# Key and value columns of the compressed branch, computed between the transposes of x, in a one-core Hymba-style decoder step

## Chip, core and metric

One core of a Trainium2 chip runs the whole step as one program. The metric is the device time of one execution in microseconds (us), the median over repeated runs. TensorE (PE in the profile) does matrix products and transposes, VectorE (DVE) and ScalarE (ACT) do elementwise work, GpSimd (POOL) does elementwise work and issues gathers, and SyncE (SP) issues most DMA transfers. Each engine works through its own list of instructions in order and waits on semaphores for the others.

## What is computed

The reference is one layer of a hybrid decoder for 1024 prompt tokens and for 8 samples of 4 new tokens, 1056 tokens in all. Cut to what the change touches:

```python
u = rmsnorm(x, lw['norm_mix'])            # x (tokens, 1024): u = x * r * norm_mix, r one number per token
z = u @ w_in                              # 2328 columns: q | k_cmp | v_cmp | k_slc | v_slc | ... | rg | rx
kc = compress(concat(cache k_cmp, k_cmp)) # blocks of 32 tokens, a small MLP per block; the same for v_cmp
h, conv_state, h_last = rglru(rx, ...)    # convolution, two gates, a linear scan over time
x = x + concat(rmsnorm(attention), rmsnorm(gelu(rg) * h)) @ w_out
v = rmsnorm(x, lw['norm_mlp'])
x = x + square(relu(v @ w_up)) @ w_down
```

`k_cmp` and `v_cmp` are columns 512 to 639 and 640 to 767 of `w_in`.

## The kernel before, in words

Tokens lie along the free axis in three chunks of 352 columns (`CH`), features along the 128 partitions. Every large product is done with three matmuls (`mm3`, lines 122 to 124), since both factors are split into a high and a low part (`split`, lines 127 and 128): high by high, high by low, low by high. An input projection of 128 columns is therefore 3 chunks of 8 blocks of features of 3 matmuls, 72 in all, and each writes 128x352.

**The start.** `fetch_x` loads x in nine tiles of up to 128 tokens (`xt`, line 276, eight buffers). `load_x` takes them in three groups of three tiles. For each of the 8 blocks of features (`kb`) it transposes the three tiles on TensorE into one PSUM tile `ps_x` (line 257), ScalarE writes the high part `u_hi` (line 261), VectorE the low part `u_lo` (line 262) and one of the two a plain copy `xr` (line 265), which GpSimd's queue stores. The factor r per token is not in u; `norm_x` builds it as a row `R` over all tokens (line 1168 makes diagonals `dg`, line 1169 broadcasts them with TensorE into `ps_bc`, line 1171 copies), and each projection multiplies its result by `R` when it leaves PSUM.

**Then, before the change:** `z_tile` runs twice, for the columns of k_cmp and of v_cmp, all three chunks of the one and then of the other. `cmp_cached` compresses the cached pages: for 4 pairs of samples and k, v it takes page data `lpg` (half loaded by SP, line 547, half gathered by GpSimd's queue, line 551; 16 tiles in three buffers), reorders it into `lpr` (line 586), transposes it on TensorE (`ps_ct`, line 593), splits it into `xj0` (k) or `xj1` (v) on ScalarE and VectorE (lines 508 and 509) and multiplies by the compression weights (`ps_c`). `kv_cmp` does the same for the new rows, and `rglru` follows.

**Weights.** `w_tile` loads 512 KB of `w_in` into `wraw` (line 299, one buffer) and splits it into `wh`, `wl`, of which there are two sets, used in turn. So the load of a third tile can be split only when the first tile's last matmul is done, and the load after that can start only when that split is done.

```python
raw = self.wrp.tile([128, KT, 128], F32, tag="wraw", name="wraw", bufs=1)
self.wp = self.wps[self.par]
self.par ^= 1
```

**Order.** The program is written with a tile library whose scheduler, at build time, sets the order on each engine from a model of the durations; the order in which the code emits operations is only a priority. `w_tile` raises it.

**Two later places.** `rglru` ends with a transpose `ps_l` of its last states (line 411). In the first eighth of the MLP, `scale_x1` sums squares of x per chunk on ScalarE and GpSimd, adds over partitions on TensorE (`ps_ms`, line 1227), makes `dg` on VectorE (line 1238), broadcasts (`ps_bc`, line 1239) and multiplies x by the result (line 1338).

Of the kernel before, what the change touches and what calls it, by code (L numbers as in the profile page):

```python
# [9 lines left out]
F32 = mybir.dt.float32  # L10
# [8 lines left out]
D = 1024  # L19
# [86 lines left out]
class K:  # L106
# [130 lines left out]
    def load_x(self):  # L237
# [7 lines left out]
        for grp in range(3):  # L245
# [6 lines left out]
            for kb in range(KT):  # L252
                pool, tag = ((self.ps_tp, "tp"), (self.ps_mm, "mm"))[kb % 2]
                ps = pool.tile([128, 512], F32, tag=tag, name="ps_x")
                o = 0
                for xt, n in tiles:
                    nc.tensor.transpose(ps[:, o : o + n], xt[:n, kb * 128 : kb * 128 + 128], self.ident[:n, :n])
                    o += n
                g = self.g_mix[:, kb : kb + 1]
                hi, lo = uh[:, kb, c0 : c0 + wdt], ul[:, kb, c0 : c0 + wdt]  # L260
                nc.scalar.activation(hi, ps[:, :wdt], AF.Copy, scale=g)
                nc.vector.scalar_tensor_tensor(lo, ps[:, :wdt], g, hi.bitcast(F32), ALU.mult, ALU.subtract)
                if kb % 2 == 0:
                    xr = self.xrp.tile([128, 2, 384], F32, tag="xr", name="xr", bufs=5)
                (nc.scalar.copy if kb % 4 == 0 else nc.vector.tensor_copy)(xr[:, kb % 2, :wdt], ps[:, :wdt])
                if kb % 2:
                    self.stores[grp, kb] = nc.gpsimd.dma_start(self.xT[kb - 1 : kb + 1, :, c0 : c0 + wdt].rearrange("k p t -> p k t"), xr[:, :, :wdt])

    def fetch_x(self):
# [3 lines left out]
        for t in range(9):  # L273
            n = 128 if t < 8 else 32
            xt = self.xtp.tile([128, D], F32, tag="xt", name="xt", bufs=8)
            nc.sync.dma_start(xt[:n], a["x_prompt"][0, t * 128 : t * 128 + 128] if t < 8 else xs)
# [28 lines left out]
    def in_proj(self, c0, evac, order=range(NCH)):  # L305
# [3 lines left out]
        for c in order:  # L309
            ps = self.ps_mm.tile([128, 512], F32, tag="mm", name="ps_in")  # L310
            sl = slice(c * CH, c * CH + CH)
            for k in range(KT):
                self.mm3(ps[:, :CH], wh[:, k], wl[:, k], uh[:, k, sl], ul[:, k, sl], k == 0, k == KT - 1)
            evac(c, ps[:, :CH])

    def z_tile(self, c0, pool, tag, bufs, scale=None, w=TOK):
# [38 lines left out]
    def rglru(self, f, c_rx):  # L355
# [52 lines left out]
        P.tensor_copy(lt[:, 27:28], h[:, SEQ - 1 : SEQ])  # L408
        P.tensor_copy(lt[:, 28:36], hs[:, :, 3])
        ps = self.ps_tp.tile([128, 512], F32, tag="tp", name="ps_l")  # L410
        nc.tensor.transpose(ps[:36, :128], lt, self.ident)
        V.tensor_copy(self.last[:, f * 128 : f * 128 + 128], ps[:36, :128])
        return h

    def rg_gate(self, f, c_rg, h):

        V, S = self.nc.vector, self.nc.scalar
        rp = self.rp
        hs = h[:, SEQ:XC].rearrange("p (s w) -> p s w", w=7)[:, :, 3:7]
        z = self.z_tile(c_rg, self.rx, "X", 4, w=XW)  # L420
        q = rp.tile([128, TOK], F32, tag="gq", name="gq", bufs=1)
        S.activation(q, z, AF.Square, scale=0.044715 ** 0.5)
# [785 lines left out]

    def chunk_ms(self, pool, xs, nf, c, ps, name):

        nc = self.nc
        acc = pool.tile([128, CH], F32, tag="sq", name="sq", bufs=3)
        for f, x in enumerate(xs):
            if f == 0:
                nc.scalar.activation(acc, x, AF.Square)
            else:
                t = pool.tile([128, CH], F32, tag="sq", name="sqt", bufs=3)
                nc.scalar.activation(t, x, AF.Square)
                nc.gpsimd.tensor_tensor(acc, acc, t, ALU.add)
        return self.sum_ms(acc, nf, ps, name)  # L1220

# [104 lines left out]

    def scale_x1(self, c):

        nc = self.nc
        x1 = self.x1  # L1330
        sl = slice(c * CH, c * CH + CH)
        pool = self.scp
        new = lambda nm: self.ps_tp.tile([128, 512], F32, tag="tp", name=nm)
        ms = self.chunk_ms(pool, [x1[:, d, sl] for d in range(8)], D, c, new("ps_ms"), "ms_v")
        M = pool.tile([128, CH], F32, tag="M", name="M", bufs=1)
        self.chunk_bcast(ms, new("ps_bc"), M)
        for d in range(8):
            nc.vector.tensor_tensor(x1[:, d, sl], x1[:, d, sl], M, ALU.mult)
        nc.vector.scalar_tensor_tensor(self.eps2[:, c], ms, D * EPS, ms, ALU.mult, ALU.mult)

    def mlp(self, PP, WU):
# [16 lines left out]
        def down(d, c, ws, hs):  # L1358
# [5 lines left out]
            V.tensor_tensor(x1[:, d, sl], x1[:, d, sl], ps[:, :CH], ALU.add)  # L1364

        for g in range(8):
            hs = []
            for fi in range(4):
                wh, wl = up_w(g * 4 + fi)
                if g == 0 and fi:  # L1370
                    self.scale_x1(CO[fi - 1])
                hh = hp.tile([128, TOK], F32R, tag="hh", name="hh", bufs=4)
                hl = hp.tile([128, TOK], F32R, tag="hl", name="hl", bufs=4)
                for c in (CO if g == 0 else range(NCH)):
# [6 lines left out]
                    V.tensor_tensor(r, r, r, ALU.mult)  # L1381
                    self.split(hh[:, sl], hl[:, sl], r)
                hs.append((hh, hl))
            ws = []
# [85 lines left out]
    def run(self):  # L1470
# [10 lines left out]
        with ExitStack() as PA:  # L1481
# [3 lines left out]
            with ExitStack() as s:  # L1485
# [3 lines left out]
                self.wrp = self.pool(WB, "wrp", side="right")  # L1489
                self.par = 0  # L1490
                with ExitStack() as s2:
                    self.xtp = self.pool(s2, "xtp")
# [7 lines left out]
                    self.vectors()  # L1500
                self.zp = self.pool(s, "zp")
                self.ctp0 = self.pool(s, "ctp0", 1)
                self.ctp1 = self.pool(s, "ctp1", 1)
                self.rowp0 = self.pool(s, "rowp0", 1)
                self.norm_x()
                zs = [self.z_tile(512 + i * 128, self.zp, "z", 2) for i in range(2)]
                self.cmp_cached()
                self.kv_cmp(zs)
        with ExitStack() as PB:
# [128 lines left out]
```

## Time and profile before

| what | value |
|---|---|
| median of 3 runs | 1540.94 us (1536.79 to 1542.21) |
| the profiled execution | 1544.62 us, its span 1542.9 us |
| TensorE busy | 1468.0 us, 95% of the span, 9445 matmuls |
| VectorE, ScalarE, GpSimd busy | 58%, 40%, 28% |
| granted TensorE clock, mean | 0.973 of full speed |

The profile comes from one execution. Times in rows are microseconds from the start of its span unless marked ns. A row of the timeline has start, duration, engine, line and operation, and in brackets the idle time before it and what released it. The duration of a matmul includes its way through the array, so its pace is read from the distance of two starts. The granted clock of TensorE is 1.00 at 2.4 GHz and 0.50 at 1.2 GHz.

### The profile page before, as it was taken

The page shows a single profiled execution, that of the slowest core. Times are in us where ns is not written, and L with a number is a line of the kernel's source. Part 1 is how long each engine was busy: PE and PEld are TensorE (multiplying, and loading weights), DVE is VectorE, ACT ScalarE, POOL GpSimd, SP SyncE. Part 2 cuts the span into 40 slices and gives each one's busy share as a digit, 9 for nine tenths or more (in the row PEclk, how much of TensorE's full clock was granted, in tenths as well). Part 3 has the DMA queues.
Part 4 walks back from the last instruction along what each step waited for, and adds up shares of the span by engine and source line. Part 5 has one row for each costly group of instructions (what it writes and reads, how often), then busy time and mean ns, then how long its engine had stood idle before and what let it go on. Part 6 is the DMA issues. An engine that isn't in the chain of part 4 may idle for free.

```text
span 1542.9 us, 24576 instructions
## 1 busy us (share of the span) xinstructions
PE 1468.0 (95%) x9445; PEld 1378.4 (89%) x9445; DVE 895.2 (58%) x1671; ACT 615.1 (40%) x1216; POOL 439.6 (28%) x533
## 2 busy tenths in 40 slices
PE   4989999999899989999999999999999999999997
PEld 3879998899877657777999999999999999999997
DVE  6664788557678868988786343433424343342445
ACT  6253775122467758767362030311203031130322
POOL 6651143342566648756580000000000000000022
PEclk8899999999789999999999999999999999999999
DMA  9554412453134100003221020511102021020102
GB/s 291 160 160 114 128 33 63 143 186 106 42 105 142 42 1 1 28 1 126 83 69 42 16 81 15 188 31 54 57 8 89 14 70 40 28 81 3 42 23 90
DMA packets 127961, 115.53 MB, mean 75 GB/s; under 512 B 16752, under 2 KB 115760, under 8 KB 127716
## 3 DMA queue, kind: packets, MB, share of 16 engines
q1 hardware_dynamic: 122446, 102.10, 21.8%
q0 software_dynamic: 3200, 8.67, 1.8%
q10 hardware_dynamic: 2198, 3.20, 0.7%
q8 instruction: 74, 1.21, 0.3%
q14 instruction: 43, 0.35, 0.1%
HBM read 98.17 MB, written 28.32 MB: 82 GB/s over the span
## 4 chain that ended last, share of the span: by engine, by line
PE 54%; DVE 4%; ACT 1%; POOL 1%; issue 1%; DMA 0%; DVEq 0%; ACTq 0%; POOLq 0%
PE ps_dn L122 8%; PE ps_dn L123 8%; PE ps_dn L124 8%; PE ps_up L122 7%; PE ps_up L123 7%; PE ps_up L124 7%; PE ps_T L1092 2%; PE ps_O L1101 1%; PE ps_O L1102 1%; PE ps_S L1060 1%; PE ps_S L1061 1%; PE ps_out L122 1%; PE ps_out L124 1%; PE ps_out L123 1%; PE ps_f L1433 0%
## 5 line engine op out<-in xcount | busy, mean ns | idle before, releaser
L122 PE MATMUL ps_up<-v_hi,wuh 128*128 128x352 f32 x768 | 248.9, 324 | 0.0
L122 PE MATMUL ps_dn<-hh,wdh 128*128 128x352 f32 x768 | 248.4, 324 | 0.0
L123 PE MATMUL ps_up<-v_lo,wuh 128*128 128x352 f32 x768 | 247.2, 322 | 0.0
L124 PE MATMUL ps_up<-v_hi,wul 128*128 128x352 f32 x768 | 246.9, 321 | 0.0
L123 PE MATMUL ps_dn<-hl,wdh 128*128 128x352 f32 x768 | 246.0, 322 | 0.0
L124 PE MATMUL ps_dn<-hh,wdl 128*128 128x352 f32 x768 | 245.7, 321 | 0.0
L1364 DVE TENSOR_TENSOR x<-x,ps_dn 128x352 f32<-128x352 f32 x192 | 99.1, 520 | 222.6 <-PE ps_dn L124 222.4
L1429 POOL TENSOR_TENSOR facc<-facc,fsq 128x352 f32<-128x352 f32 x18 | 17.0, 942 | 701.8 <-ACT fsq L1427 701.6
L127 ACT CAST wdh<-wd 128x1024 fp32r<-128x1024 f32 x32 | 33.5, 1048 | 342.2 <-PE ps_dn L123 288.7
L123 PEld LDWEIGHTS ps_up<-v_lo,wuh 128*128 128x128 f32 x768 | 145.0, 189 | 0.0
L122 PEld LDWEIGHTS ps_up<-v_hi,wuh 128*128 128x128 f32 x768 | 144.6, 188 | 0.0
L124 PEld LDWEIGHTS ps_up<-v_hi,wul 128*128 128x128 f32 x768 | 144.5, 188 | 0.0
L123 PEld LDWEIGHTS ps_dn<-hl,wdh 128*128 128x128 f32 x768 | 144.3, 188 | 0.0
L122 PEld LDWEIGHTS ps_dn<-hh,wdh 128*128 128x128 f32 x768 | 144.1, 188 | 0.0
L124 PEld LDWEIGHTS ps_dn<-hh,wdl 128*128 128x128 f32 x768 | 144.0, 188 | 0.0
L122 PE MATMUL ps_in<-u_hi,wh 128*128 128x352 f32 x432 | 142.0, 329 | 0.0
L124 PE MATMUL ps_in<-u_hi,wl 128*128 128x352 f32 x432 | 140.6, 326 | 0.0
L123 PE MATMUL ps_in<-u_lo,wh 128*128 128x352 f32 x432 | 140.4, 325 | 0.0
L128 DVE TENSOR_TENSOR ptl<-ps_T,pth 128x512 fp32r<-128x512 f32 x132 | 88.1, 683 | 16.3 <-ACT pth L127 14.9
L127 ACT CAST pth<-ps_T 128x512 fp32r<-128x512 f32 (+1 forms) x148 | 84.1, 586 | 30.7 <-PE ps_T L1092 25.2
L127 ACT CAST hh<-r 128x352 fp32r<-128x352 f32 x96 | 46.7, 487 | 92.3 <-DVE r L1381 91.5
L122 PEld LDWEIGHTS ps_in<-u_hi,wh 128*128 128x128 f32 x432 | 82.4, 191 | 0.6 <-issue 0.3
(511 smaller groups left out, 3266.7 us busy)
## 6 DMA issues: line engine op xcount, KB each, us to landing
wu<-in_w_up_dram SPq DMA_DIRECT2D x32, 512.0 KB
wd<-in_w_down_dram SPq DMA_DIRECT2D x32, 512.0 KB
wraw<-in_w_in_dram SPq DMA_DIRECT2D x18, 512.0 KB
slc_dram<-in_cache_kv_dram SPq DMA_DIRECT2D x64, 128.0 KB
kvs<-slc_dram SPq DMA_DIRECT2D x32, 256.0 KB
xres<-xT_dram SPq DMA_DIRECT2D x8, 528.0 KB
x_dram<-xres SPq DMA_DIRECT2D x8, 528.0 KB
x<-x_dram SPq DMA_DIRECT2D x3, 1408.0 KB
```

The lines of the kernel that those rows point to most:

```text
L122: t.matmul(out, wh, xh, start=first, stop=False)
L123: t.matmul(out, wh, xl, start=False, stop=False)
L124: t.matmul(out, wl, xh, start=False, stop=last)
L127: self.nc.scalar.copy(hi, src)
L128: (eng or self.nc.vector).tensor_tensor(lo, src, hi.bitcast(F32), ALU.subtract)
L1060: T.matmul(pv, qr[:, h], kh[:, ks], start=True, stop=False)
L1061: T.matmul(pv, qr[:, h], kl[:, ks], start=False, stop=not (far or dia))
L1092: T.transpose(ps[:K, h * 128 : h * 128 + 128], src(h), self.ident)
L1101: T.matmul(O, v, ph, start=first, stop=False)
L1102: T.matmul(O, v, pl, start=False, stop=last)
L1364: V.tensor_tensor(x1[:, d, sl], x1[:, d, sl], ps[:, :CH], ALU.add)
L1429: P.tensor_tensor(acc, acc, sq, ALU.add)
```

## The change

`kv_chunk(c)` computes chunk c of both tiles. Chunks 0 and 1 are emitted after the second and third group of transposes, copied out of PSUM by ScalarE without R, and multiplied by R on GpSimd later, 704 columns at once; chunk 2 comes where the two `z_tile` calls were. The result pool `zp` is opened earlier, the x tiles get six buffers in place of eight, and half of the transposes use the PSUM pool `ps_c` in place of `ps_mm`. Apart from that, `ps_l` is emitted in the next stage, and `scale_x1` becomes a generator whose steps are emitted one per chunk of the MLP's first products.

```diff
-                pool, tag = ((self.ps_tp, "tp"), (self.ps_mm, "mm"))[kb % 2]
+                pool, tag = ((self.ps_tp, "tp"), (self.ps_c, "c"))[kb % 2]
...
+            if grp:
+                self.kv_chunk(grp - 1)
...
-            xt = self.xtp.tile([128, D], F32, tag="xt", name="xt", bufs=8)
+            xt = self.xtp.tile([128, D], F32, tag="xt", name="xt", bufs=6)
...
+    def kv_chunk(self, c):
+
+        nc = self.nc
+        if c == 0:
+            self.wkv = [self.w_tile(512 + i * 128, 128) for i in range(2)]
+            self.zkv = [self.zp.tile([128, TOK], F32, tag="z", name="z", bufs=2) for _ in range(2)]
+        uh, ul = self.u
+        sl = slice(c * CH, c * CH + CH)
+        for z, (wh, wl) in zip(self.zkv, self.wkv):
+            ps = self.ps_mm.tile([128, 512], F32, tag="mm", name="ps_in")
+            for k in range(KT):
+                self.mm3(ps[:, :CH], wh[:, k], wl[:, k], uh[:, k, sl], ul[:, k, sl], k == 0, k == KT - 1)
+            if c < 2:
+                nc.scalar.copy(z[:, sl], ps[:, :CH])
+            else:
+                nc.vector.tensor_tensor(z[:, sl], ps[:, :CH], self.R[:, sl], ALU.mult)
+                nc.gpsimd.tensor_tensor(z[:, : 2 * CH], z[:, : 2 * CH], self.R[:, : 2 * CH], ALU.mult)
...
-                zs = [self.z_tile(512 + i * 128, self.zp, "z", 2) for i in range(2)]
+                self.kv_chunk(2)
                 self.cmp_cached()
-                self.kv_cmp(zs)
+                self.kv_cmp(self.zkv)
...
+        for c in CO:
+            sl = slice(c * CH, c * CH + CH)
+            acc = self.squares(pool, [x1[:, d, sl] for d in range(8)])
+            yield
+            yield
+            ms = self.sum_ms(acc, D, new("ps_ms"), "ms_v")
+            yield
...
+        steps = self.scale_x1()
...
-                if g == 0 and fi:
-                    self.scale_x1(CO[fi - 1])
...
+                    if g == 0 and (fi or c != CO[0]):
+                        next(steps, None)
```

What the scheduler makes of it is seen in the order of the instructions. The order differs up to the gates of the attention and in the first eighth of the MLP; in the attention between them it is the same.

On TensorE at the start (`ps_x` are transposes of x, `ps_in` the columns of k_cmp and v_cmp), before and then changed:

```order
L257 MATMUL ps_x<-ident,xt 128x128 x2
L170 MATMUL ps_gm<-ident,gm 128x8
L257 MATMUL ps_x<-ident,xt 128x128 x2
L459 MATMUL ps_pe<-ident,pe 128x16
L257 MATMUL ps_x<-ident,xt 128x128 x6
L459 MATMUL ps_pe<-ident,pe 128x16
L525 MATMUL ps_pg<-pf_143,tok 128x32
L257 MATMUL ps_x<-ident,xt 128x128 x35
```

```order
L257 MATMUL ps_x<-ident,xt 128x128 x8
L549 MATMUL ps_pg<-pf_146,tok 128x32
L257 MATMUL ps_x<-ident,xt 128x128 x5
L122 MATMUL ps_in<-u_hi,wh 128x352
L123 MATMUL ps_in<-u_lo,wh 128x352
L124 MATMUL ps_in<-u_hi,wl 128x352
L122 MATMUL ps_in<-u_hi,wh 128x352
L123 MATMUL ps_in<-u_lo,wh 128x352
L124 MATMUL ps_in<-u_hi,wl 128x352
L122 MATMUL ps_in<-u_hi,wh 128x352
L257 MATMUL ps_x<-ident,xt 128x128 x3
L123 MATMUL ps_in<-u_lo,wh 128x352
```

Before, all 72 transposes stand ahead of the first `ps_in`; now matmuls begin after 15 transposes and alternate with them to the end of x: 18 matmuls and 18 transposes, then 26 matmuls in a row, and so on.

On ScalarE at the end of the x stage (`wh` is the high part of the next weight tile, `xj0h` and `xj1h` the high parts of the first cached k and v), before and then changed:

```order
L127 CAST wh<-wraw 128x1024
L508 CAST xj1h<-peT 128x8x2
L1171 COPY R<-ps_bc 128x32
L508 CAST xj1h<-ps_ct 128x8x2x32 x2
L508 CAST xj0h<-ps_ct 128x8x2x32
L127 CAST wh<-wraw 128x1024
L508 CAST xj1h<-ps_ct 128x8x2x32 x2
```

```order
L532 CAST xj0h<-ps_ct 128x8x2x32 x3
L127 CAST wh<-wraw 128x1024
L1195 COPY R<-ps_bc 128x512
L222 ACTIVATE sp_w<-sp_w 128x4
L1195 COPY R<-ps_bc 128x32
L127 CAST wh<-wraw 128x1024
L532 CAST xj1h<-peT 128x8x2
L532 CAST xj1h<-ps_ct 128x8x2x32 x2
L532 CAST xj0h<-ps_ct 128x8x2x32
```

The two `wh` casts, with the four `xj0h` casts ahead of the second before, now follow each other closely, and the fourth `xj0h` stands behind both.

On SP, where the loads of weight tiles 4 and 5 (`wraw`) stand among the page loads (`lpg`), before and then changed:

```order
L547 DMA lpg<-in_cache_kv_dram 64x2x256
L299 DMA wraw<-in_w_in_dram 128x8x128
L537 TENSOR_LOAD pt
L537 ISA x2
L537 TENSOR_LOAD pt
L537 ISA x2
L547 ISA
L547 DMA lpg<-in_cache_kv_dram 64x2x256
```

```order
L561 TENSOR_LOAD pt
L561 ISA x2
L301 DMA wraw<-in_w_in_dram 128x8x128 x2
L571 ISA
L571 DMA lpg<-in_cache_kv_dram 64x2x256
```

Before, 14 page loads stand ahead of the first of these two `wraw` and 20 ahead of the second; now 12 stand ahead of both, and the other 20 behind.

## Rows read from the trace of the kernel before

**Rows 1.** The page, part 1: busy time, share of the span, instructions.

```profile
PE 1468.0 (95%) x9445; PEld 1378.4 (89%) x9445; DVE 895.2 (58%) x1671; ACT 615.1 (40%) x1216; POOL 439.6 (28%) x533
```

**Rows 2.** Stretches: length, busy by engine (instructions), then TensorE's clock, DMA share, GB/s.

```profile
14.90:43.40 28.50, 16.27 (x67) 11.11 (x67) 26.62 (x71) 21.78 (x46) 20.17 (x25) 0.64 1.01 268
43.40:47.00 3.60, 3.60 (x14) 3.60 (x13) 3.60 (x16) 1.53 (x2) 3.11 (x6) 0.50 1.03 285
47.00:73.30 26.30, 25.50 (x167) 24.98 (x167) 13.29 (x30) 4.58 (x9) 15.94 (x20) 1.00 0.44 138
...
833.00:1500.00 667.00, 667.00 (x4204) 666.86 (x4203) 251.89 (x439) 138.42 (x236) 6.32 (x7) 1.00 0.16 48
```

**Rows 3.** What TensorE waited for, 0 to 45 us: total, times, longest.

```profile
PE ps_x L257 <- issue: 6.0, 1, 6.0
PE ps_x L257 <- DVE xr L265: 4.4, 5, 1.8
```

**Rows 4.** Timeline of TensorE, first 75 us.

```profile
13.56 1.33 PE L257 MATMUL ps_x<-ident,xt 128*128 128x128 f32 x5
...
31.98 4.13 PE L257 MATMUL ps_x<-ident,xt 128*128 128x128 f32 x15 [5.99 <-issue]
...
44.10 0.49 PE L124 MATMUL ps_in<-u_hi,wl 128*128 128x352 f32 x1
...
46.16 0.49 PE L122 MATMUL ps_in<-u_hi,wh 128*128 128x352 f32 x1
...
73.32 1.04 PE L593 MATMUL ps_ct<-ident,lpr 128*128 128x128 f32 x8
74.11 0.37 PE L122 MATMUL ps_c<-xj0h,cwkh 128*128 128x258 f32 x1
```

**Rows 5.** Timeline of ScalarE: a weight cast, casts of cached rows, and a cast in the MLP.

```profile
73.35 1.05 ACT L127 CAST wh<-wraw 128x1024 fp32r<-128x1024 f32 x1 [6.88 <-PE ps_in L123]
74.31 1.07 ACT L508 CAST xj1h<-ps_ct 128x512 fp32r<-128x512 f32 x2
...
975.13 1.05 ACT L127 CAST wdh<-wd 128x1024 fp32r<-128x1024 f32 x1 [4.87 <-DMA wd<-in_w_down_dram]
```

**Rows 6.** Timeline of VectorE: a small multiply, and the split of a weight tile.

```profile
28.34 3.50 DVE L211 TENSOR_SCALAR hb<-vec 128x8 f32<-128x8 f32 x1
...
61.28 1.22 DVE L128 TENSOR_TENSOR wl<-wraw,wh 128x1024 fp32r<-128x1024 f32 x1 [0.42 <-ACT wh L127]
```

**Rows 7.** Timeline of SP's DMA issues.

```profile
50.57 4.12 SPq L547 DMA_DIRECT2D lpg<-in_cache_kv_dram  x4
62.53 0.41 SPq L299 DMA_DIRECT2D wraw<-in_w_in_dram  x1
...
79.07 17.36 SPq L547 DMA_DIRECT2D lpg<-in_cache_kv_dram  x12
...
971.54 12.06 SPq L1389 DMA_DIRECT2D wd<-in_w_down_dram  x3
```

**Rows 8.** Timeline of GpSimd: a tensor operation, and the last gather.

```profile
29.46 2.36 POOL L128 TENSOR_TENSOR cwkl<-cwraw,cwkh 128x1024 fp32r<-128x1024 f32 x1
...
100.68 0.95 POOL L551 DMA_INDIRECT lpg<-in_cache_kv_dram,idx  x1 [0.30 <-issue]
```

**Rows 9.** What TensorE waited for in the recurrent stage, 120 to 420 us.

```profile
PE ps_g L123 <- DVE xl L128: 2.0, 2, 1.1
PE ps_g L122 <- ACT xh L127: 1.3, 1, 1.3
...
PE ps_g L122 <- ACT t L391: 1.1, 1, 1.1
```

**Rows 10.** Timeline of TensorE, first eighth of the MLP: broadcasts that waited.

```profile
795.23 0.68 PE L1239 MATMUL ps_bc<-dg,ones 128*128 128x128 f32 x4 [1.53 <-DVE dg L1238]
...
814.24 0.68 PE L1239 MATMUL ps_bc<-dg,ones 128*128 128x128 f32 x4 [3.16 <-DVE dg L1238]
```

**Rows 11.** The stretch just behind the second of those waits.

```profile
815.00:818.00 3.00, 3.00 (x12) 3.00 (x11) 1.90 (x6) 1.27 (x3) 0.00 (x0) 0.51 0.56 159
```

More of the change, by code (lines that the diff above doesn't have):

```diff
@@ L409, in rglru, with rglru_last @@
         P.tensor_copy(lt[:, 28:36], hs[:, :, 3])
+        return h, lt
+    def rglru_last(self, f, lt):
         ps = self.ps_tp.tile([128, 512], F32, tag="tp", name="ps_l")
-        nc.tensor.transpose(ps[:36, :128], lt, self.ident)
-        V.tensor_copy(self.last[:, f * 128 : f * 128 + 128], ps[:36, :128])
-        return h
+        self.nc.tensor.transpose(ps[:36, :128], lt, self.ident)
+        self.nc.vector.tensor_copy(self.last[:, f * 128 : f * 128 + 128], ps[:36, :128])
     def rg_gate(self, f, c_rg, h):
@@ L418, in rg_gate @@
         rp = self.rp
+        h, lt = h
         hs = h[:, SEQ:XC].rearrange("p (s w) -> p s w", w=7)[:, :, 3:7]
         z = self.z_tile(c_rg, self.rx, "X", 4, w=XW)
+        self.rglru_last(f, lt)
         q = rp.tile([128, TOK], F32, tag="gq", name="gq", bufs=1)
@@ L1207, in rnn_proj, with squares @@
                 nc.sync.dma_start(self.x1D[d], xt)
-    def chunk_ms(self, pool, xs, nf, c, ps, name):
+    def squares(self, pool, xs):
         nc = self.nc
@@ L1219, in chunk_ms @@
                 nc.gpsimd.tensor_tensor(acc, acc, t, ALU.add)
-        return self.sum_ms(acc, nf, ps, name)
+        return acc
     def sum_ms(self, acc, nf, ps, name):
@@ L1325, in mlp_v, with scale_x1 @@
             self.nc.vector.scalar_tensor_tensor(self.vl[:, d, sl], x1[:, d, sl], g, self.vh[:, d, sl].bitcast(F32), ALU.mult, ALU.subtract)
-    def scale_x1(self, c):
+    def scale_x1(self):
         nc = self.nc
         x1 = self.x1
-        sl = slice(c * CH, c * CH + CH)
         pool = self.scp
         new = lambda nm: self.ps_tp.tile([128, 512], F32, tag="tp", name=nm)
[L1334 to L1339, printed above, removed]
+        for c in CO:
[5 more added lines that the diff above has]
+            yield
+            M = pool.tile([128, CH], F32, tag="M", name="M", bufs=1)
+            self.chunk_bcast(ms, new("ps_bc"), M)
+            for d in range(8):
+                nc.vector.tensor_tensor(x1[:, d, sl], x1[:, d, sl], M, ALU.mult)
+            nc.vector.scalar_tensor_tensor(self.eps2[:, c], ms, D * EPS, ms, ALU.mult, ALU.mult)
     def mlp(self, PP, WU):
@@ L1490, in run @@
                 self.par = 0
+                self.zp = self.pool(s, "zp")
                 with ExitStack() as s2:
@@ L1500, in run @@
                     self.vectors()
-                self.zp = self.pool(s, "zp")
                 self.ctp0 = self.pool(s, "ctp0", 1)
```

## Prediction

> **What bounds the kernel now.** I read the page's busy times first. TensorE is busy for 95% of the span, the next engine for 58% [rows 1], so a change pays where TensorE stands idle or runs slowly, and nowhere else. The stretches say where that is [rows 2]. From 833 to 1500 us TensorE is busy for all of 667 us with 4204 matmuls, 0.159 us each, at a clock of 1.00: nothing is to be had there. In the 28.5 us from 14.9 it is busy for only 16.27, at 0.64 of the clock, while VectorE is busy for 26.62. In the 3.6 us after that it works without a break, still at 0.50, and only from 47.0 at 1.00.
>
> The waits of the first 45 us [rows 3] tell what TensorE stands for in the x stage: one gap of 6.0 us put down to issue, and 4.4 us for VectorE's plain copies `xr`, which free the PSUM tiles. The timeline of TensorE [rows 4] gives the prices at either clock. Between the rows at 44.10 and 46.16 lie seven steps: 2.06 / 7 = 0.294 us per `ps_in` matmul at the half clock, against 0.159 at full. Fifteen transposes in a row took 4.13 us, 0.275 each; eight at full clock 1.04, 0.13 each. The last `ps_in` ends at about 73.3, and the first `ps_c`, the real work of the next stage, starts at 74.11.
>
> **The sum's base.** The profiled execution took 1544.62 us, 3.7 above the median of 1540.94. The saving is worked out in the profile and taken off the median.
>
> **Added and removed work.** TensorE does the same matmuls. ScalarE gets four copies of 128x352 in place of four of VectorE's multiplies, and GpSimd two multiplies of 128x704. The nearest row for these is a tensor operation of 128x1024, 2.36 us [rows 8]: 704 / 1024 of it is 1.6 us, 3.3 for both. They come after the last chunk and are wanted only by `kv_cmp`, behind the cached pages, so the compression of the pages covers them; without that cover they would cost the 3.3. In that row VectorE shows an effect: while GpSimd worked on `cwkl` at 29.46, a VectorE operation on 128x8 took 3.50 us [rows 6, 8]. The Trainium skill (SBUF — State Buffer, "Who interferes with whom") says that the two engines share a port pair under an exclusive lock; that pair of rows agrees, and by it the new multiplies would also hold VectorE for up to 3.3 us. VectorE is busy for 13.29 of the 26.3 us after 47 [rows 2], so I take nothing for it.
>
> Six x tiles in place of eight: tiles 7 to 9 can be loaded only when the first group's transposes are done, at about 15 us, and are wanted at about 31. Loads there ran at 268 GB/s [rows 2], by which three tiles of 512 KB take 6 us. Nothing, if nothing else stands ahead in SP's queue; 3 us at worst.
>
> **Term A, the start.** From 14.9 the new order has 57 transposes and 144 `ps_in` matmuls to do, with matmuls between the groups in the time in which TensorE stood for VectorE and for issue. All at the half clock: 57 x 0.275 + 144 x 0.294 = 58, so the end is at 73, with the broadcasts of R 76. All at the full clock: 57 x 0.13 + 144 x 0.159 = 30.3, end at 45, with broadcasts and early `ps_ct` (3.4 together, by their rows after 47) 49. VectorE's 26.62 us of splits don't shrink, so 49 would already be tight. Where between? The row at 31.98 shows 4 us of back-to-back transposes that stayed at half; the row at 44.10 shows dense matmuls that came to full at 47, 3.6 us after they began [rows 2, 4]. In the new order the first stretch alternates 18 matmuls with 18 transposes; I take the half clock for that (10.2, to 25.1) and for 12 matmuls of the run of 26 behind it (3.6, as before, to 28.7). The rest, 39 x 0.13 + 114 x 0.159 = 23.2, and 3.4 for the broadcasts and `ps_ct`, ends at **55** in place of 73.3.
>
> The Trainium skill (TensorE: Matmul & The Clock Gate, Part 1) says that the throttled clock is the default and that sustained activity releases it. The matmuls at 47 agree and the transposes at 32 do not; by the rule the clock would rise in the first alternating stretch, and T would lie nearer 49 than 55 (rival 2 below has its time and chance).
>
> Not all of these 18 us arrive. The next weight tile waits for the second set, which is free only with the last `ps_in`. Before, the first wait of this kind was hidden: its load and split came while the second tile was still being multiplied, and `wh` at 73.35 followed the last matmul at once [rows 5]. Now tiles 4 and 5 stand next to each other on SP, and on ScalarE both casts stand ahead of the fourth `xj0h`. After the end at 55 follow: `wh` 1.05 [rows 5], `wl` 1.22 [rows 6], the next load, bounded by the `wd` load issued at 971.54 and used at 975.13, 3.6 [rows 5, 7], `wh` again 1.05, and three casts of cached rows at 0.5 each, 1.5 [rows 5]. That is 8.4: the first `ps_c` at **63.4** in place of 74.1. Meanwhile TensorE has only some 16 `ps_ct` (2.1 us) and broadcasts to do. It goes idle for some 6 us, and comes back at half clock: behind a wait of 3.16 us in the MLP, twelve matmuls took the 3.00 us in which 19 would go at 0.159 [rows 10, 11], 1.1 to 1.3 us lost. Four fewer `ps_ct` are done by then (0.5). Gain: 10.7 - 0.5 - 1.3 = 8.9.
>
> The page gathers come next. SP issued its last twelve page loads in 17.36 us, 1.45 each, from 79.07 to 96.4, and earlier four in 4.12, 1.03 each [rows 7]; GpSimd's last gather started at 100.68 [rows 8]. Now 12 loads are out before SP is held by the two `wraw` up to the second split, at about 64; twenty more end between 84.6 and 93, which is 3.4 to 11.8 earlier than 96.4, where TensorE wants 9. I take 1 off: **A = 8**. Its ends: -9 with the half clock throughout and the hand-over behind it (below), +24 for an end at 49 without the stall.
>
> **Term B, the gates.** The order at the end of the recurrent stage changes, so the waits of `ps_g` there (2.0, 1.3, 1.1 [rows 9]) may be filled with other products. They are 4.4 in all; which part goes the rows can't tell. With `ps_l` out of the way, VectorE and ScalarE still make `xl` and `xh` at the same pace. I take +1.5, a third; ends -3 (a new wait as long as the present ones) and +4.4.
>
> **Term C, the MLP's first eighth.** `ps_bc` waits 1.53 and 3.16 for `dg` [rows 10], with the half clock behind the second [rows 11]: 4.7 + 1.3 = 6 to be had, 6.7 with the small rest of that stretch. But VectorE still has to get to `dg` between its multiplies and weight splits, and TensorE has about as many matmuls ahead of it as before. I take +1; ends -2 and +6.7.
>
> **Sum.** 8 + 1.5 + 1 = 10.5: 1534.1 for the profiled execution, **1530.4** against the median, 0.7% less. A measurement of this kernel can tell about 0.5%, 7.7 us, from no change.
>
> **Rivals.**
>
> *1. The pages set the pace.* The gain at the start is kept only if the page data come earlier too. For it: at 1.45 us per load the last one is just 3.4 us earlier, and a stage that runs ahead of its gathers waits for them. Against it: SP's 17.36 us held waits for buffers, which come free sooner. Then A is 3.5, the sum 3 to 6, the time about **1536**, within 0.5%. Chance 0.22.
>
> *2. The clock rises early, or the hand-over is covered.* Without the 6 us of idle time and its half clock A is 8 + 7.3; with an end at 50, A is 13. With B and C 16 to 20: about **1523**. For it: TensorE has more work in the stretch than before, without the gap of 6.0. Against it: VectorE's 26.62 us, and the order of ScalarE's casts. Chance 0.18.
>
> *3. The half clock persists.* Slower than before: transposes kept the clock at 0.50 for the 28 us to 43.4 [rows 2, 4], and now they alternate with matmuls to the end of x. If that mixture holds the clock down, 144 matmuls pay 0.294, the last `ps_in` is at 76, the first `ps_c` 8.4 behind, at 84.4 in place of 74.1: 10.3 lost, less 2.5 from B and C, about **1549**. It decides from an end of `ps_in` beyond 66: 66 + 8.4 = 74.4, no gain. Against it: the runs of 26 matmuls are longer than the 12 that sufficed at 43.4. Chance 0.07.
>
> *4. The moves later on lose.* `ps_l` or the steps of `scale_x1` push TensorE into longer waits: -3 from B and -2 from C in place of +2.5, with A at 8, gives +3: about **1538**, within 0.5%. Chance 0.08.
>
> **How the numbers follow.** My forecast has 0.45. Its own range is 1526 to 1534. Faster by over 0.5% means below 1533.2: most of the forecast (0.40) and rival 2 (0.18), 0.58. Slower is rival 3 and a little of 4, 0.08. The rest is 0.34. The range takes in rivals 1, 4 and most of 2 and leaves out rival 3: 1519 to 1541.
>
> **What would show it.** Right: the first `ps_in` at about 15 us; `ps_in` steps of 0.16 us from about 29; the last at 55; an idle time of some 6 us ahead of the first `ps_c` at 63, released by ScalarE's `wh` behind a `wraw` load; the last gather at some 92; the first `ps_r` of the next stage some 8 us earlier. Wrong: steps of 0.294 us past 45; gaps in the x stage put down to x loads (six tiles too few); `ps_ct` or `ps_c` waiting for `lpr` at 75 to 100 (rival 1); `ps_bc` waits of over 2 us in the MLP's first eighth together with more `ps_g` waits (rival 4).

## The result, and the profile after

The change is slower: 1548.72 us median of 9 runs (1544.39 to 1556.84) against 1537.69 for the kernel before (9 runs, 1536.12 to 1542.21), a ratio of 1.0059 with a 95% interval of 1.0042 to 1.0076. That is some 9 us; the two medians lie 11 us apart. The forecast was 1530.4, with a range that ended at 1541.

The two profiled executions hide this. The profiled execution of before took 1544.62 us, more than all nine timed ones, that of the change 1544.39, the least of its nine, and their spans differ by 0.3 us. So the stages are compared below over several profiles, and a single profile is read for mechanisms, not for sums.

The page of the change, part 1, is nearly that of before [rows 1]: TensorE is busy for 1462.6 us, VectorE for 895.1, ScalarE for 617.0 and GpSimd for 446.7.

The stretches tell more. The columns are those of [rows 2]. Each row is one stage, cut at the first matmul of the next: to the first `ps_c` (cached pages), to the first `ps_r` (new rows), to `ps_st` (recurrent stage), to `ps_gt` (gates), to `ps_S` (attention). Before:

```profile
0.00:74.10 74.10, 51.45 (x272) 44.15 (x273) 46.54 (x127) 35.25 (x67) 47.68 (x67) 0.84 0.78 232
74.10:115.20 41.10, 36.91 (x298) 33.04 (x297) 28.39 (x63) 23.63 (x56) 19.31 (x36) 1.00 0.51 152
115.20:148.00 32.80, 31.76 (x208) 29.34 (x206) 13.63 (x33) 13.09 (x36) 2.61 (x10) 0.90 0.37 101
148.00:268.60 120.60, 116.11 (x718) 114.19 (x718) 96.69 (x132) 81.02 (x119) 39.66 (x47) 1.00 0.27 77
268.60:407.20 138.60, 135.46 (x852) 131.13 (x850) 83.69 (x145) 29.91 (x40) 45.23 (x38) 0.99 0.38 125
```

The change:

```profile
0.00:65.70 65.70, 45.75 (x268) 39.85 (x269) 45.83 (x119) 36.71 (x71) 44.44 (x61) 0.96 0.82 237
65.70:118.10 52.40, 42.28 (x301) 37.27 (x300) 29.61 (x67) 24.38 (x55) 26.89 (x44) 0.88 0.50 144
118.10:153.70 35.60, 33.27 (x205) 30.83 (x203) 13.42 (x33) 12.84 (x35) 2.33 (x10) 0.86 0.36 99
153.70:273.70 120.00, 116.11 (x721) 114.53 (x721) 97.24 (x129) 79.89 (x118) 41.85 (x46) 1.00 0.26 73
273.70:412.90 139.20, 135.36 (x852) 131.26 (x850) 85.03 (x147) 31.35 (x42) 45.20 (x39) 0.99 0.40 129
```

The start is 8.4 us shorter; the forecast had 10.7. The next stage, with nearly the same matmuls (301 and 298), is 11.3 us longer. About half of that is waiting and half is pace: TensorE stands idle for 10.1 us there (52.40 - 42.28) in place of 4.2, and at 0.88 of the clock in place of 1.00 the matmuls keep it busy for 42.28 us in place of 36.91.

TensorE's timeline shows how the start went (it answers to [rows 4]):

```profile
14.57 0.50 PE L124 MATMUL ps_in<-u_hi,wl 128*128 128x352 f32 x1
...
15.74 0.50 PE L122 MATMUL ps_in<-u_hi,wh 128*128 128x352 f32 x1
...
22.31 0.32 PE L123 MATMUL ps_in<-u_lo,wh 128*128 128x352 f32 x1
...
25.03 0.32 PE L122 MATMUL ps_in<-u_hi,wh 128*128 128x352 f32 x1
...
52.67 0.32 PE L124 MATMUL ps_in<-u_hi,wl 128*128 128x352 f32 x1
...
56.22 1.53 PE L617 MATMUL ps_ct<-ident,lpr 128*128 128x128 f32 x12
64.94 1.11 PE L617 MATMUL ps_ct<-ident,lpr 128*128 128x128 f32 x4 [7.20 <-DVE xj1l L533]
65.71 0.56 PE L122 MATMUL ps_c<-xj0h,cwkh 128*128 128x258 f32 x1
66.07 1.06 PE L617 MATMUL ps_ct<-ident,lpr 128*128 128x128 f32 x4
70.31 0.58 PE L123 MATMUL ps_c<-xj0l,cwkh 128*128 128x258 f32 x1 [3.18 <-DVE xj0l L533]
70.69 0.42 PE L124 MATMUL ps_c<-xj0h,cwkl 128*128 128x258 f32 x1
...
74.35 0.42 PE L123 MATMUL ps_c<-xj0l,cwkh 128*128 128x258 f32 x1
...
74.76 0.29 PE L122 MATMUL ps_c<-xj0h,cwkh 128*128 128x258 f32 x1
74.88 0.28 PE L123 MATMUL ps_c<-xj0l,cwkh 128*128 128x258 f32 x1
```

Four steps from 14.57 to 15.74 are 0.29 us each, the half clock; seventeen from 22.31 to 25.03 are 0.16, the full one. The columns are complete at 53.0 us, before at 73.3. Between 12.3 and 53.0 us TensorE is hardly ever idle:

```profile
12.30:53.00 40.70, 39.02 (x234) 34.55 (x233) 31.97 (x76) 25.82 (x54) 28.68 (x35) 1.00 0.96 262
```

Then TensorE waits 7.20 us, does eight transposes and one `ps_c` matmul (at 65.71), waits 3.18 more, and the real work of the stage begins at 70.3, at the half clock again: seventeen steps from 70.69 to 74.35 are 0.215 us each, where the step from 74.76 to 74.88 is 0.12.

What it waited for stands on other engines. ScalarE waits for the second weight tile and is done with the fourth `xj0h` at 63.4. VectorE has some twenty operations to do between 56.82 and 63.0, most of them on 128x4 for the recurrent stage, so it splits that weight tile (`wl`) 1.2 us after `wh` is there; `xj1l`, for which TensorE waits, stands behind `wl`. SP is held by the two weight loads up to 64.6, and the page loads behind them land only at 69.4, where both VectorE and GpSimd wait for them. The last `xj0l`, TensorE's second wait, has its `xj0h` since 63.4, but in VectorE's list it stands behind the copy of a page into `lpr`, which waits for its load (timelines of ScalarE, SP, VectorE and GpSimd; they answer to [rows 5, 7, 8]):

```profile
60.79 1.04 ACT L127 CAST wh<-wraw 128x1024 fp32r<-128x1024 f32 x1 [4.28 <-DMA wraw<-in_w_in_dram]
...
62.80 0.60 ACT L532 CAST xj0h<-ps_ct 128x512 fp32r<-128x512 f32 x1
```

```profile
37.92 9.44 SPq L571 DMA_DIRECT2D lpg<-in_cache_kv_dram  x6
56.92 7.68 SPq L301 DMA_DIRECT2D wraw<-in_w_in_dram  x2
64.92 39.33 SPq L571 DMA_DIRECT2D lpg<-in_cache_kv_dram  x20
```

```profile
56.82 1.66 DVE L223 TENSOR_SCALAR sp_s<-sp_w 128x4 f32<-128x4 f32 x1
...
63.00 1.21 DVE L128 TENSOR_TENSOR wl<-wraw,wh 128x1024 fp32r<-128x1024 f32 x1
...
64.21 1.27 DVE L533 TENSOR_TENSOR xj1l<-ps_ct,xj1h 128x512 fp32r<-128x512 f32 x2
69.36 0.29 DVE L610 COPY lpr<-lpg 128x256 f32<-128x256 f32 x1 [3.88 <-DMA lpg<-in_cache_kv_dram]
69.57 0.69 DVE L533 TENSOR_TENSOR xj0l<-ps_ct,xj0h 128x512 fp32r<-128x512 f32 x1
```

```profile
55.73 4.36 POOL L334 TENSOR_TENSOR z<-z,R 128x704 f32<-128x704 f32 x2 [1.33 <-ACT R L1195]
...
69.42 0.49 POOL L610 COPY lpr<-lpg 128x256 f32<-128x256 f32 x1 [6.47 <-DMA lpg<-in_cache_kv_dram]
...
106.88 1.04 POOL L575 DMA_INDIRECT lpg<-in_cache_kv_dram,idx  x1 [0.30 <-DMA lpg<-in_cache_kv_dram]
```

The last twenty page loads took SP 39.33 us, to 104.3 (before: to 96.4 [rows 7]); the last gather started at 106.88 (before 100.68 [rows 8]). What SP waited for with its page loads, 48 to 125 us, before and then changed:

```profile
SPq L547 <- DVE lpr L586: 3.1, 3, 1.5
...
SPq L547 <- POOL lpr L586: 1.4, 2, 0.9
```

```profile
SPq L571 <- DVE lpr L610: 6.9, 2, 6.5
...
SPq L571 <- POOL lpr L610: 5.9, 3, 3.6
```

These are waits for a page buffer, which is free when its `lpr` copies are done: 12.8 us in place of 4.5 (in the second profiles below, 12.1 in place of 2.7).

At the two later places these are the waits of TensorE, from 120 to 420 us and in the MLP's first eighth (they answer to [rows 9, 10]; the MLP's three waits of `ps_bc` were 5.2 us in all before):

```profile
PE ps_g L122 <- ACT xh L127: 1.9, 1, 1.9
PE ps_bc L1193 <- DVE dg L1192: 1.9, 4, 1.4
PE ps_g L123 <- DVE xl L128: 1.1, 1, 1.1
...
PE ps_l L434 <- POOL lt L429: 0.8, 2, 0.6
```

```profile
PE ps_bc L1263 <- DVE dg L1262: 4.8, 3, 3.0
```

### The profile page after: what moved, and what is told of

It is laid out like the page before. It is cut to its first block, busy times and chain, and to the rows that moved or that the text cites. A ratio compares the mean times of both kernels' runs of the same rounds, so it can differ in the third digit from the quotient of the medians.

```text
span 1542.6 us, 24571 instructions
## 1 busy us (share of the span) xinstructions
PE 1462.6 (95%) x9445; PEld 1374.3 (89%) x9445; DVE 895.1 (58%) x1667; ACT 617.0 (40%) x1220; POOL 446.7 (29%) x535
## 4 chain that ended last, share of the span: by engine, by line
PE 54%; DVE 3%; POOL 2%; ACT 1%; issue 1%; DMA 1%; DVEq 0%; SPq 0%; POOLq 0%; ACTq 0%
PE ps_dn L122 8%; PE ps_dn L123 8%; PE ps_dn L124 8%; PE ps_up L122 7%; PE ps_up L123 7%; PE ps_up L124 7%; PE ps_T L1116 1%; PE ps_O L1126 1%; PE ps_O L1125 1%; PE ps_S L1084 1%; PE ps_S L1085 1%; PE ps_out L122 1%; PE ps_out L124 1%; PE ps_out L123 1%; PE ps_f L1463 0%
```

## Experiments

### Is the loss real, and which part makes it

`e5_before_again` and `e6_after_again` are the two kernels unchanged.

> The kernel before, unchanged, as a kernel of its own: what two sets of runs of the same program differ by. If the losses of 0.5 to 0.7% of the change and of its parts are real: ratio 1.000, its interval holds 1. Rival N (sets of runs on a chip differ by that much anyway): ratio 1.004 or more.

> The change, unchanged, a second set of runs and a second profile. If the loss is real: ratio 1.004 to 1.008, and the profile again shows TensorE idle ahead of the first ps_c and at the half clock from about 61 to 75 us. Rival N: the ratio may lie anywhere from 0.998 to 1.008, and the half clock elsewhere.

Measured: before against itself 1.0002 (0.9986 to 1.0017), the change 1.0068 (1.0046 to 1.0090). The loss is real, and a ratio of about 1.002 can be told from none. The second profile of the change has the same two waits, 7.2 and 3.2 us.

`e1_kv_only` is the change with the old `scale_x1` and the old place of `ps_l`; `e2_rest_only` has these two alone, `e7_last_only` only `ps_l`, `e8_scale_only` only `scale_x1`:

```diff
# e7: before, with
+    def rglru_last(self, f, lt):
...
     z = self.z_tile(c_rg, self.rx, "X", 4, w=XW)
+    self.rglru_last(f, lt)
# e8: before, with
+        steps = self.scale_x1()
...
+                    if g == 0 and (fi or c != CO[0]):
+                        next(steps, None)
```

> Only kv_chunk, its pools and the six x tiles; the gates of the recurrent stage and the MLP's first eighth as before. Theory S (the whole loss is made in the first 145 us, where SP holds the page loads behind two weight loads): the same loss as the change, some 6 to 9 us slower than before. Rival L (the moves later on lose): within 2 us of before, or faster.

> Only ps_l and the steps of scale_x1 emitted later; the start as before. Theory S: within 2 us of before. Rival L: 5 us or more slower than before. The forecast's terms B and C would give 2.5 us faster.

> Only ps_l emitted in the next stage. Theory G (the reordered gates of the recurrent stage cost): 4 us or more slower than before, with more waits of ps_g or ps_in between 150 and 260 us. Rival M (it is the MLP's first eighth): within 2 us of before. Forecast: 1.5 us faster.

> Only the steps of scale_x1 emitted later; the order differs in 24 rows on TensorE, all in the MLP's first eighth. Theory G: within 2 us of before. Rival M: 4 us or more slower, with more idle time or half clock between 775 and 835 us. Forecast: 1 us faster.

Measured: e1 1.0064 (1.0045 to 1.0084), e2 1.0047 (1.0030 to 1.0064), e7 1.0048 (1.0030 to 1.0066), e8 0.9993 (0.9975 to 1.0011). So the start alone loses as much as the whole change, moving `ps_l` alone loses 7 us too, where the forecast's term B had 1.5 us gained, and `scale_x1` does nothing that can be told. The parts don't add up; each changes the order that the scheduler makes elsewhere, and e7 has another order in the attention as well, which the change has not.

Where the time goes is read from the stages of eight profiles (us, cut as above; the last column from the first `ps_up` to the first `ps_dn`):

| kernel | to `ps_c` | to `ps_r` | to `ps_st` | to `ps_gt` | to `ps_S` | to `ps_up` | to `ps_dn` |
|---|---|---|---|---|---|---|---|
| before | 74.1 | 41.1 | 32.8 | 120.6 | 138.6 | 368.3 | 57.3 |
| e5, before | 73.9 | 45.0 | 32.8 | 120.7 | 136.7 | 363.5 | 57.3 |
| e8, `scale_x1` | 73.3 | 44.5 | 32.8 | 120.7 | 137.2 | 367.2 | 56.8 |
| the change | 65.7 | 52.4 | 35.5 | 120.0 | 139.2 | 363.1 | 56.8 |
| e6, the change | 65.0 | 62.1 | 33.9 | 120.3 | 140.7 | 366.3 | 56.9 |
| e1, start only | 66.3 | 56.1 | 37.6 | 119.8 | 142.9 | 369.1 | 57.4 |
| e2, both later places | 73.9 | 44.2 | 31.2 | 120.3 | 140.0 | 369.6 | 56.8 |
| e7, `ps_l` | 73.0 | 46.9 | 32.8 | 120.2 | 141.1 | 371.0 | 57.5 |

Up to the first `ps_st` the first three need 150.1 us in the mean, the next three 158.2: 8 us lost, although the first `ps_c` comes 8 us earlier. The recurrent stage gains 0.6, the gates lose 3.4 (137.5 to 140.9), the attention is even (366.3 and 366.2), the MLP's eighth gains 0.5 where `scale_x1` is changed. Together 10 us, about what the runs show.

In e7 the recurrent stage, where theory G looked, is no longer than before. Its gates and its attention are, but one profile doesn't tell how its 7 us divide. On TensorE the gates have the order of before in e5 and e8. In the other five kernels 16 of the 850 matmuls stand elsewhere, in e1 too, which leaves `ps_l` in its old place.

The gates lose between the first `ps_gt` and the first `ps_bc`. One row each of the stretch view, for before, the change and e7:

```profile
268.60:287.10 18.50, 17.23 (x113) 14.55 (x111) 14.60 (x31) 6.11 (x9) 5.12 (x2) 1.00 0.43 160
```

```profile
273.70:294.00 20.30, 18.35 (x113) 16.03 (x111) 16.86 (x35) 7.49 (x11) 5.09 (x2) 0.92 0.50 179
```

```profile
272.90:295.10 22.20, 19.83 (x113) 17.27 (x110) 17.94 (x35) 7.04 (x11) 5.08 (x2) 0.85 0.44 162
```

The same 113 matmuls, some of them narrow (18 write one column, 9 write 24), take 18.5, 20.3 and 22.2 us; in the other order TensorE waits a little more and its clock is at half for a part of them. Whether the waits bring the clock down was not tried.

### Is it SP's order, or GpSimd's multiplies

`e3_pages_first` has the weight loads from the fourth on behind the last page load, `e4_r_late` has GpSimd's multiplies in `kv_cmp`.

```diff
# e3
+            if self.held:
+                st.enter_context(self.tc.issue_after(self.sp_loads[31].ins))
             nc.sync.dma_start(raw[:, :, :m], src)
# e4
-                nc.gpsimd.tensor_tensor(z[:, : 2 * CH], z[:, : 2 * CH], self.R[:, : 2 * CH], ALU.mult)
...
         for i, z in enumerate(zs):
+            nc.gpsimd.tensor_tensor(z[:, : 2 * CH], z[:, : 2 * CH], self.R[:, : 2 * CH], ALU.mult)
```

> The change, with the loads of weight tiles 4 and on issued by SP behind the last of the 32 page loads. Theory S: the 7.2 us for xj1l and the 3.2 us for xj0l at 65 to 70 us vanish, and with them most of the half clock from 61 to 75 us; the first ps_r comes 8 to 14 us earlier than in the change, and the time is 2 to 8 us below before. Rival P (GpSimd's gathers set the pace of the pages, whatever SP does): the first ps_r moves by under 3 us and the time stays above before.

> The change, with GpSimd's two multiplies by R emitted in kv_cmp, behind the cached pages, in place of at 55.7 us, where they took 4.36 us ahead of two gathers. Theory S: at most 1 us faster than the change, since those gathers are not what the first ps_c waits for. Rival P: 3 to 5 us faster than the change.

Measured: e3 1.0062 (1.0041 to 1.0083), e4 1.0071 (1.0047 to 1.0095). In e3 the wait of 7.2 us became 4.4 and that of 3.2 went, but others came (one of 3.5 us for `xj1h`), and the first `ps_r` came at 118.0, as in the earlier of the change's two profiles (118.1 and 127.0). Its page loads were no longer held by weights, but now waited 16.8 us for VectorE's `lpr` copies, that is for page buffers. So SP's hold was one link only: taken away, the buffers held. The result is the one that rival P named. Its reason, the pace of GpSimd's gathers, is neither shown nor excluded: in e3's trace six gathers stand in a row on GpSimd from 77.73 to 85.0 us, and `lpr` copies behind them in the same list. e4 is no faster than the change, so the multiplies are not the cause.

### Do the pages set the pace

`e9_nopages_before` and `e10_nopages_after` load and gather only the first three of the 16 page tiles:

```diff
-                        lp = self.lsp.tile([128, 2, 2, 256], F32, tag="lpg", name="lpg", bufs=3)
+                        nth = b * 4 + s2 * 2 + gh
+                        if nth < 3:
+                            lps.append(self.lsp.tile([128, 2, 2, 256], F32, tag="lpg", name="lpg", bufs=3))
+                        lp = lps[nth % 3]
```

> The kernel before with only the first three of the 16 page tiles loaded and gathered, and used again for the other 13 (26 of 32 loads and 26 of 32 gathers are left out; reorders, transposes, splits and products stay). It sets the base for the next kernel: what the stage of the cached pages takes when no page is waited for, counted to the first ps_st of the recurrent stage (at 148 to 152 us in the kernel before).

> The change with the same 26 loads and 26 gathers left out. Theory P (the pages pace the stage, through their buffers and the queues of SP and GpSimd): the first ps_st comes 6 us or more earlier than in the kernel before without these pages. Rival H (the stage is paced by its own splits, or by the half clock after the hand-over, whatever the pages do): within 3 us of it, or later.

Measured: e9 1546.25 us (ratio to before 1.0042, 1.0024 to 1.0060), e10 1536.26 (0.9987, 0.9970 to 1.0003). The change is 10 us faster once no page is waited for. (e9 is slower than before although it does less; its order is another, so only the pair is compared.) Stretches to the first `ps_st`, e9 and then e10:

```profile
0.00:60.60 60.60, 38.49 (x199) 31.63 (x199) 41.55 (x121) 33.84 (x65) 34.30 (x53) 0.80 0.84 258
60.60:107.10 46.50, 46.06 (x361) 43.86 (x359) 30.64 (x67) 23.14 (x53) 7.97 (x23) 1.00 0.40 120
107.10:147.60 40.50, 40.50 (x285) 37.97 (x283) 17.82 (x41) 15.84 (x41) 2.10 (x11) 1.00 0.30 82
```

```profile
0.00:54.90 54.90, 44.83 (x263) 38.49 (x263) 35.35 (x99) 34.36 (x66) 32.60 (x53) 1.00 0.92 275
54.90:98.70 43.80, 38.47 (x298) 34.73 (x296) 34.47 (x86) 24.37 (x56) 10.54 (x25) 0.96 0.41 121
98.70:139.20 40.50, 40.50 (x286) 37.94 (x284) 17.89 (x41) 15.89 (x41) 2.10 (x11) 1.00 0.37 101
```

The first `ps_st` comes at 139.2 against 147.6, 8.4 us earlier, and behind it the two take the same time to 1 us. This shows the cause of the loss up to `ps_st`: the change saves TensorE those 8 us, and the supply of pages takes them back. Rival H falls with it, since splits and products are all there and the clock in e10's stage is 0.96. Two limits remain. The scheduler gives both kernels some 70 more `ps_in` matmuls ahead of the first `ps_st` than before and the change have, so the 8.4 us belong to this pair. And loads, gathers and the reuse of buffers are left out together, so the pair does not say which of them holds.

### Which link of the supply, and can the gain be kept

`f4_after_lpg4` is the change with a fourth page buffer in place of an x tile, `f2_lpg4_nolast` the same with `ps_l` in its old place (its text was written behind that of f1, which is its "one before it"), `e11_lpg4` the change with the fourth buffer and the weight loads behind the pages, `f1_pf_lpg4_nolast` that with `ps_l` in its old place, `g1_lpg4_last_end` with all `ps_l` at the stage's end, `g2_pages_last_end` as g1 with three buffers, `f3_before_lpg4` the kernel before with four buffers and the changed `scale_x1`.

```diff
# e11, f1, f2, f4, g1 (f3: xt 8 to 7)
-            xt = self.xtp.tile([128, D], F32, tag="xt", name="xt", bufs=6)
+            xt = self.xtp.tile([128, D], F32, tag="xt", name="xt", bufs=5)
...
-                        lp = self.lsp.tile([128, 2, 2, 256], F32, tag="lpg", name="lpg", bufs=3)
+                        lp = self.lsp.tile([128, 2, 2, 256], F32, tag="lpg", name="lpg", bufs=4)
# g1, g2
-        self.rglru_last(f, lt)
+        self.lts.append(lt)
...
     def rglru_out(self):
+        for f, lt in enumerate(self.lts):
+            self.rglru_last(f, lt)
```

> The change with the weight loads behind the page loads, and a fourth page buffer in the place of the sixth x tile. Theory P: the first ps_st comes 3 us or more earlier than with three buffers (152 to 164 us in the change and its variants so far). Rival H: within 2 us of the same kernel with three, 153 us.

> The change with the fourth page buffer in the place of the sixth x tile, and nothing else. Theory B: the first ps_st at 147 to 150 us in place of 153 to 161, the time 3 to 7 us below the change. Rival Q: within 2 us of the change.

> As the one before it, but with the weight loads where the scheduler puts them. Theory B (the number of page buffers sets the pace): the first ps_st as early as with the loads held, 147 to 150 us. Rival Q (SP's hold on the page loads does): 152 us or later.

> The kernel of the fourth page buffer (weight loads behind the pages), with ps_l back in its old place. There the two waits of ps_l for GpSimd's lt took 5.2 us in the recurrent stage. Theory L (that loss came from ps_l's new place): the stretch from the first ps_st to the first ps_gt falls from 126 to 120 to 122 us, and the time is at or up to 3 us below before. Rival W (it came from the weight loads behind the pages): it stays at 125 us or more.

> The kernel before with a fourth page buffer in the place of the eighth x tile, and the steps of scale_x1 later. Theory B: TensorE's work up to the first ps_r fills the time there but for 5 us, so that at most these are gained, 0 to 4 us faster than before. If it gains as much as the change loses by its three buffers (6 us or more), the fourth buffer and not the order of the products is what matters.

> The kernel with the fourth page buffer and the weight loads behind the pages, with all four ps_l emitted at the end of the recurrent stage, where no product stands behind one that waits for lt. In that kernel ps_l in its changed place waited 5.2 us, 4.4 of it at once. If that is what the recurrent stage lost: the stretch from the first ps_st to the first ps_gt falls from 126 to 120 to 122 us and the time is 0 to 4 us below before, the first version that beats both. If the order of the gate products is (ps_g waited 4.9 us with ps_l in its old place): 124 us or more, and the time 3 us or more above before.

> The same with three page buffers, the weight loads behind the pages. Against the kernel with ps_l in the changed place, 1550.7 us mean span: within 3 us, since its recurrent stage took 121 us already; the first ps_st again at 151 to 155 us.

| kernel | buffers | weight loads held | first `ps_st` | to `ps_gt` | to `ps_S` | ratio (95%) |
|---|---|---|---|---|---|---|
| e3 | 3 | yes | 153.2 | 121.1 | 142.8 | 1.0062 (1.0041 to 1.0083) |
| g2 | 3 | yes | 152.1 | 119.7 | 144.5 | 1.0054 (1.0035 to 1.0073) |
| f4 | 4 | no | 155.9 | 120.5 | 140.3 | 1.0077 (1.0051 to 1.0102) |
| f2 | 4 | no | 156.9 | 120.0 | 140.3 | 1.0055 (1.0035 to 1.0075) |
| e11 | 4 | yes | 147.7 | 126.4 | 135.7 | 1.0036 (1.0020 to 1.0053) |
| f1 | 4 | yes | 151.8 | 125.0 | 140.1 | 1.0085 (1.0059 to 1.0111) |
| g1 | 4 | yes | 146.9 | 123.4 | 142.9 | 1.0083 (1.0058 to 1.0108) |
| f3 (products as before) | 4 | no | 150.0 | 124.3 | 136.6 | 1.0019 (1.0001 to 1.0036) |

Neither link alone brings the first `ps_st` under 152 us; both together bring it to 146.9, 147.7 and 151.8. So theory B (the buffers alone) did not come out, and SP's order alone did not either. That each takes over from the other fits, but these are single profiles, and two of the change lie 7.3 us apart here (153.6 and 160.9). And none of these kernels beats the one before; f3, expected 0 to 4 us faster, is not faster either. What the first stages gained in e11, the recurrent stage lost (126.4 against 120 to 121), where TensorE waited for `lt`:

```profile
PE ps_l L439 <- POOL lt L434: 5.2, 2, 4.4
PE ps_g L123 <- ACT xh L128: 2.2, 1, 2.2
```

With `ps_l` in its old place (f1, 125.0) or at the end (g1, 123.4) the stretch stayed long, and `ps_g` waited for `xh` 4.9 and 5.0 us instead; f1 and g1 expected 120 to 122 if `ps_l` were the reason. Why the stretch is longer stays open. It is not the four buffers alone (f4 and f2: 120.5 and 120.0) nor the held loads alone (e3 and g2: 121.1 and 119.7). `e12_chunk0` went half way:

```diff
# e12
-            if grp:
-                self.kv_chunk(grp - 1)
+            if grp == 2:
+                self.kv_chunk(0)
...
+                self.kv_chunk(1)
                 self.kv_chunk(2)
```

> Only chunk 0 of both tiles between the transposes of x, behind the third group; chunks 1 and 2 where the two z_tile calls were, and R for chunk 0 on VectorE. Theory P: TensorE has 96 matmuls, 15 us, left to cover the page loads after the end of x, so that the idle time ahead of the first ps_c and the half clock there are gone; the first ps_st no later than in the kernel before, 148 to 152 us, and the total within 3 us of before. Rival H: half clock and idle time in the stage of the pages as in the change, the total 4 us or more above before.

Measured: 1.0075 (1.0050 to 1.0101), the first `ps_st` at 154.4, no earlier than in the change, with 8.7 us idle and a clock of 0.84 in the stage of the pages, as rival H had it. The 96 matmuls left were no cover; theory P's picture of a single stall that 15 us of work would hide was too simple. That the chain paces the whole stage fits this, but e12 alone doesn't show it.

## Why the prediction was wrong

**The x stage ended where the text put it, partly by luck.** Its end was put at 55; it came at 53.0. The clock rose at about 16.6 us and not at 28.7, after TensorE had worked without a break from 11.8. There rival 2 had the better guess. The Trainium skill (TensorE: Matmul & The Clock Gate, Part 1) says that sustained activity releases the throttle, and the rise at 16.6 agrees; the transposes before, 9 us from 31.98 with 0.4 us of idle time among them, stayed at half and do not. For a full clock from the start the text had 49, so some 4 us of work were missing from its sum. They were not VectorE's splits, which it took as the limit: TensorE was busy for 39.02 of the 40.70 us and waited 0.6 for VectorE. Its prices came from long runs of one kind; where the kinds alternate, the first `ps_in` behind transposes took 0.24 to 0.26 us to the next start, for 0.159, which is a part of it. Rival 3 (half clock to the end of x) was wrong.

**The hand-over was the right mechanism, too small, on another path.** It was to take 8.4 us, with the first `ps_c` at 63.4, released by ScalarE. ScalarE was done at 63.4. But TensorE waited for VectorE, of whose list the text had only `wl`: the first `ps_c` came at 65.7, and the next at 70.3. The text counted the second weight tile and stopped there. It left out the page load issued behind that tile at 64.9, which landed at 69.4, and the `lpr` copy of that page, behind which `xj0l` stood. The half clock behind it cost 17 x (0.215 - 0.12) = 1.6 us in these first steps, forecast 1.3.

**The step that failed is the page term of A.** It took off 1 us for the pages, from "twenty more end between 84.6 and 93". They ended at 104.3: 1.97 us each, not 1.03 to 1.45. Those prices were taken from rows in which the buffers came free sooner; SP's loads waited 4.5 us for `lpr` copies before and 12.8 in the change. The chain closes on itself: the loads wait for `lpr` copies, the copies for TensorE's `ps_ct` and for page data, `ps_ct` for the splits, and the splits stand behind page copies in VectorE's list. In place of 8 us gained, 8 were lost up to the first `ps_st`: some 8 gained up to the first `ps_c`, where the forecast had 10.7, and some 16 given back. About half of what the stage of the pages grew by is TensorE at the half clock, for which the text had 1.3 us.

Rival 1 named the pages and priced them at 3.5 us gained, bounding them by their own rate; nothing said that the stage could become longer than before. Its sign, `ps_ct` or `ps_c` waiting for `lpr`, did not show: TensorE's waits there are put down to VectorE's `xj0l` and `xj1l`, with the page copies hidden ahead of them. Without waits for pages the pair e9 and e10 gains 8.4 us up to `ps_st` and 10 in all, about the forecast's own A of 8 and sum of 10.5.

**Term B** had the recurrent stage right in sign (0.6 gained, not 1.5), but e1, without the move of `ps_l`, gains as much there. It did not look at the next stage, where the gates take 3.4 us more, in e1 as well. **Term C** was 0.5, not 1: VectorE's `dg` is as late as ever, 4.8 us of waits for 5.2. Both moves were priced as local; e7 shows that moving one transpose changes the order as far as the attention, and that kernel is 7 us slower.

**GpSimd's multiplies** took 4.36 us for an estimate of 3.3. VectorE worked beside them, and its 128x4 operation at 56.82 took 1.66 us. The Trainium skill (SBUF — State Buffer, "Who interferes with whom") describes an exclusive lock on the port pair that the two engines share; these two rows agree. It is not what the change loses by, since e4, with the multiplies later, is no faster.

## What to carry to other kernels

Before moving TensorE's work earlier, ask what that work was covering: here the two column tiles hid the loads, gathers and copies of the next stage, and with the cover gone that chain, not TensorE's work, set the stage's end. Price a chain of transfers in the state that it will have (queue blocked, few buffers free), not at the rate of its best rows. Where a scheduler sets the order, measure each part of a change alone, because a small move in one stage reorders others.

## What the runs showed of the hardware

TensorE's clock was the unexpected part of the bill. Over all their executions the kernel before ran at a mean granted clock of 0.979 (e5, 12 runs), the change at 0.971 (e6, 6 runs), although its x stage left the half clock 30 us earlier (at 16.6 in place of 47.0). The half clock had moved: into the stage of the pages (0.88 and 0.79 in two profiles of the change, 1.00 and 0.96 in two of before) and into the gates (1.00 before, 0.92 and 0.85 in the rows above). In those rows the slower matmuls cost more than the longer gaps: 1.1 against 0.7 us in the change, 2.6 against 1.1 in e7.

The record of the granted clock can begin late. In the kernel before the transposes from 13.56 us on ran at the pace of the half clock (five in 1.33 us, where eight took 1.04 at 73.32 [rows 4]), but this row, 16 to 18 us, shows 1.00, and 0.50 stands in the rows only from 24 us on:

```profile
16.00:18.00 2.00, 1.45 (x6) 1.02 (x7) 2.00 (x5) 2.00 (x6) 0.53 (x1) 1.00 1.29 252
```

So the 0.64 that [rows 2] have for 14.9 to 43.4 us is too high, as is the 1.00 of the change's row from 12.30 us, and early on the pace of the steps is the better witness.

And one profile is a sample: the stage from the first `ps_c` to the first `ps_r` took 52.4 us in one profile of the change and 62.1 in another, 41.1 and 45.0 in two of before. A difference of a few us in one stage needs more than one profile of each kernel.
